# Three small reorderings in a hybrid encoder layer: transposes ahead of their copies, normalised products two at a time, a norm factor left in PSUM

## The chip, the cores and the metric

The kernel runs on one core of a Trainium2 chip. A core has TensorE (matrix products, PE in the profile, its weight loads PEld), VectorE (DVE), ScalarE (ACT), GpSimd (POOL) and SyncE (SP, which here only issues transfers). TensorE writes to PSUM, eight banks of 128 partitions by 512 float32 values; VectorE and ScalarE read it there. All else lies in SBUF. Each engine works through its own queue in order, and semaphores make one wait for another. The metric is the device time of one execution in microseconds; lower is better.

## The reference

One encoder layer, batch 1, 512 positions, width 2048, all in float32:

```
xn   = rms_norm(x)                       # attn_norm_g
u_val, u_gate, q, k, v = split(xn @ w_in)
A    = silu(layer_norm(depthwise_conv31(u_val * sigmoid(u_gate))))   # 1024 channels
B    = neighbourhood attention(q, k, v)  # 16 heads of 64, 8 x 64 grid, window 8 x 16, learned bias
x    = x + concat(rms_norm(A), rms_norm(B)) @ w_out
up   = depthwise_conv3(rms_norm(x) @ w_up)        # 2 x 5632 channels
gate, val = split(up)
x    = x + (silu(gate) * val) @ w_down
out  = rms_norm(x) * final_norm_g
```

## The kernel before

Activations lie transposed: a tile holds 128 channels by 512 positions. A product in float32 accuracy is made of three on rounded parts: each operand is split into a high part (a ScalarE copy that rounds) and a low part (a VectorE subtraction), and `mm3` issues high x high (L131), high x low (L135) and low x high (L136) into one PSUM bank. Weights come as raw units of 128 x 1024, are split by `parts` (L117 on ScalarE, L121 on VectorE), and are prepared three units ahead of their use.

The program is traced in Python, and a planner then puts each engine's instructions into a fixed order: among those that its own timing takes as ready, the one traced first goes first. `pin` (keep in program order) ties an instruction behind the one traced before it on its engine. Banks and buffers are handed out by tag; a new tile waits until the readers of the buffer's last tile are done.

The stages that matter, in order:

1. The input projections (`project`, tiles named `pj`), in the order that `ORDER` gives. After each group of eight k-steps `tick` advances a generator of side work by one step. One generator, `attention`, takes two heads (a pair) at a time: load tables, scores, softmax, then `turn`, then, two steps on, `values`.
2. `turn(ts)` transposes the pair's 16 blocks of 128 x 128 softmax values on TensorE (L537), in four groups of four. Groups 2 and 3 go to a bank each of tag `tr`, groups 0 and 1 to the two halves (one bank each) of one wide tile of tag `sc`. Behind each group ScalarE copies its bank to SBUF (L542). There are eight turns. The first `mm3` traced after a turn is pinned behind it.
3. The output projection runs in two halves, `out_half(ma, read_a)` over the convolution group and `out_half(mb, after)` over attention's, 16 output tiles of 24 products each. In the first half `read_a` multiplies each finished tile by the group's norm factor (L637, tile `oa`, from PSUM) and adds it to the residual (L638). Three PSUM banks of tag `mm` take turns, so a tile's bank must be read before the third tile after it begins.
4. `norm_b` is a generator that runs on the ticks of that first half. From attention's sum of squares it makes the factor `rna` through `factor` and `spread`, and then for each of the eight tiles `i` multiplies `aos[i]` by it (L627) and splits the result into `mb` (L170 on ScalarE, L171 on VectorE). It yields once, behind `i == 4`. The second half needs all eight, from its first output tile on.
5. The gated MLP in a fast matrix product scheme (tiles `pu`), 44 hidden tiles; this is most of the time. Down products (`pd`) are added to the residual in DRAM.
6. The tail. The last residual tiles `x2` are finished for the first 384 positions (`fm`), with sums of squares in `acc`. `spread(..., "rstd3", ...)` rounds and splits `acc` (L195, L196), sums it over channels by two products with ones (L200, bank of tag `po`, named `st`), and makes the factor by a root on ScalarE (L204) and three VectorE steps (L205, L206, L207). The last step writes `rstd` in SBUF. Meanwhile TensorE makes the last 128 positions with tokens on partitions, four banks `pt` of 512 columns (L1055, L1061, L1065, L1068); each is squared and summed on ScalarE (L1071), and its gain multiplied in on VectorE (L1077).
7. `along(g, k)` is called beside these products. At (1, 0), behind that step's first product, it runs the second part of `spread`; from then on each call hands out two pairs of output tiles to `finish`. Pairs 1, 4 and 7 go through ScalarE (gain, L1014) and GpSimd (factor, L1015, stored as a pair by L1021); the five others through one VectorE instruction a tile, x times gain times factor (L1017, each tile stored by L1019). The stores stand in SP's queue in program order.
8. When the fourth square sum is there, a chain of small instructions (L1079 to L1083) makes the factor for the last 128 positions, four column blocks `xg` are scaled and stored (L1091), and the program ends.

Of the kernel before, what the change touches and what calls it, by code (L numbers as in the profile page):

```python
# [10 lines left out]
F32 = mybir.dt.float32  # L11
F32R = mybir.dt.float32r
AF = mybir.ActivationFunctionType
ALU = mybir.AluOpType
AX = mybir.AxisListType

P = 128
D = 2048
# [14 lines left out]
NP_ = HEADS // 2  # L33
# [33 lines left out]
def layer(ctx: ExitStack, tc: tile.TileContext, xT, xG, xw, w_a, w_in, w_v, w_out, w_up, w_down, par, tab, g3, out, last_out):  # L67
    nc = tc.nc
# [6 lines left out]
    psa = ctx.enter_context(tc.tile_pool(name="psa", bufs=1, space=bass.MemoryType.PSUM))  # L75
# [9 lines left out]
    def t2(name, dt=F32):  # L85
        return tp.tile([P, S], dt, tag="t2k", name=name)

    def t4(shape, name):

        return wpool.tile(shape, F32, tag="raw", name=name, bufs=NR)  # L90

    pin = tc.keep_in_program_order
# [5 lines left out]
    def pc(name, i):  # L98
        o = POFF[name] + i
        return prm[:, o:o + 1]  # L100
# [66 lines left out]
    def split(src, g, name):  # L167

        h, l = t2(name + "h", F32R), t2(name + "l", F32R)
        nc.scalar.activation(h, src, AF.Copy, scale=g)  # L170
        nc.vector.scalar_tensor_tensor(l, src, g, h.bitcast(F32), op0=ALU.mult, op1=ALU.subtract)  # L171
        return h, l
# [15 lines left out]
        nc.vector.tensor_mul(y, y, v)  # L188
        nc.vector.scalar_tensor_tensor(y, y, 1.5, r, op0=ALU.add, op1=ALU.mult)

    def spread(acc, to, n, name, bank, hold=False):

        m = to.stop - to.start
        h, l = (t2("n" + c, F32R)[:, :m] for c in "hl")
        nc.scalar.activation(h, acc[:, to], AF.Copy)  # L195
        nc.vector.tensor_sub(l, acc[:, to], h.bitcast(F32))  # L196
        yield
        ps = bank()[:, :m]
        for i, x in enumerate((h, l)):
            x = nc.tensor.matmul(ps, ones_r, x, start=i == 0, stop=i == 1)  # L200
            if hold:
                pin(x)
        r, q = t2(name)[:, :m], t2("q")[:, :m]
        nc.scalar.activation(r, ps, AF.Abs_reciprocal_sqrt, scale=1.0 / n, bias=eps)  # L204
        nc.vector.scalar_tensor_tensor(q, r, -0.5 / n, r, op0=ALU.mult, op1=ALU.mult)  # L205
        nc.vector.scalar_tensor_tensor(q, ps, n * EPS, q, op0=ALU.add, op1=ALU.mult)  # L206
        nc.vector.scalar_tensor_tensor(r, q, 1.5, r, op0=ALU.add, op1=ALU.mult)  # L207
        return r

# [5 lines left out]
    def factor(acc, n, name, rest=1, free=False):  # L215
        steps = spread(acc, slice(0, S), n, name, lambda: stat_bank(free))
        next(steps)
        for _ in range(rest):
            yield
        try:  # L220
            next(steps)
        except StopIteration as e:
            return e.value
# [39 lines left out]
    ps = psa.tile([P, 2, S], F32, tag="sc", name="idle")  # L263
# [3 lines left out]
    for k in range(KD):  # L267
        if k < CH:
            raw = t4([P, U * P], "raw")
            n = S + 2 * P + (0 if k else KD)  # L270
# [3 lines left out]
        else:  # L274
            if k % CH == 0:
                raw = t4([P, U * P], "raw")
            if k % CH == 0 or k == CH + 2:
                o, n = 2 * (k % CH) * P, 2 * (2 if k < 2 * CH else CH) * P
# [4 lines left out]
        g = g1[:, k:k + 1] if k else raw[:, n - KD:n - KD + 1]  # L283
# [17 lines left out]
    for step in ORDER:  # L301
# [5 lines left out]
        i = next(a_ if step == "a" else q_)  # L307
# [220 lines left out]

    def turn(ts):
        pts, first = {}, True  # L530
        for n in (2, 3, 0, 1):
            if n == 0:
                wide = psa.tile([P, 2, 4, P], F32, tag="sc", name="trp")
            ps = wide[:, n] if n < 2 else psa.tile([P, 4, P], F32, tag="tr", name="trp", bufs=2)
            for i in range(2):
                for ch in range(2):
                    m = nc.tensor.transpose(ps[:, 2 * i + ch, :], ts[n][:, i, ch * P:(ch + 1) * P], ident)  # L537
                    if not first:
                        pin(m)
                    first = False  # L540
            pts[n] = t2("pt").rearrange("p (c k) -> p c k", c=4)
            nc.scalar.activation(pts[n], ps, AF.Copy)  # L542
        turned.append(pts)
        return pts
# [19 lines left out]
    def attention():  # L564

        before = None
        for p in range(NP_):
            while len(qk) <= p:
                yield
            ts = tables(p)  # L570
            yield
            if before:
                values(*before)
            banks = scores(p, not before)
            softmax(banks, ts)
            yield
            yield
            yield
            pts = turn(ts)
            yield  # L580
            before = p, pts
        yield
        values(*before)

    p, n = -1, 0
# [38 lines left out]
    def norm_b():  # L624
        r = yield from factor(acc_na, NA, "rna")
        for i in range(NP_):
            nc.vector.tensor_mul(aos[i], aos[i], r)  # L627
            mb.append(split(aos[i], pc("nag", i), "mb"))
            if i == NP_ // 2:
                yield  # L630

    def read_a(d, ps):
        wait.append((d, ps))
        while ra and wait:
# [3 lines left out]
            nc.vector.tensor_add(x2[d], x2[d], t)  # L638

    steps.append(norm_b())  # L640
    assert len(ma) == NC_
    out_half(ma, read_a)
# [333 lines left out]
    n = CH  # L976
# [28 lines left out]
    fm, tm = slice(0, LT), slice(LT, S)  # L1005

    def finish(pair, r, apart=False, split=False):

        o = t4([P, 2, LT], "fin")
        for i in range(2):  # L1010
            d = 2 * pair + i
            x, g = x2[d][:, fm], pc("g3", d)
            if apart:
                nc.scalar.activation(x, x, AF.Copy, scale=g)  # L1014
                nc.gpsimd.tensor_mul(o[:, i], x, r)  # L1015
            else:
                nc.vector.scalar_tensor_tensor(o[:, i], x, g, r, op0=ALU.mult, op1=ALU.mult)  # L1017
            if split:
                nc.sync.dma_start(out[pair][:, i], o[:, i])  # L1019
        if not split:  # L1020
            nc.sync.dma_start(out[pair], o)  # L1021

    acc = t2("acc3")
    for d in range(KD):
        ps = psm.tile([P, S], F32, tag="mm", name="pd")[:, fm]
        for k in range(n):
            mm3(ps, ws[d // CH * CH + k], d % CH, hs[k][0][:, fm], hs[k][1][:, fm], k == 0, k == n - 1)
        i = nc.vector.tensor_add(x2[d][:, fm], x2[d][:, fm], ps)
# [2 lines left out]
                pin(nc.scalar.activation(idle, eps, AF.Abs_reciprocal_sqrt))  # L1031
        sum_sq(acc[:, fm], x2[d][:, fm], d == 0, to=fm)

    rows = spread(acc, fm, D, "rstd3", stat_bank, hold=True)
    next(rows)
    wide = psa.tile([P, 2, S], F32, tag="sc", name="pt")
    banks = [psa.tile([P, S], F32, tag="tr", name="pt", bufs=2) if g % 2 else wide[:, g // 2] for g in range(CH)]
    rb, xg = [], []
    sums, v, r, y, w = (sm.tile([P, CH], F32, tag="rs" + c, name="rs" + c) for c in "lvryw")
    v, r, y, w = (t[:, :1] for t in (v, r, y, w))  # L1040
    pairs = list(range(KD // 2))

    def along(g, k):
        if (g, k) == (1, 0):
            try:
                next(rows)
            except StopIteration as e:
                rb.append(e.value)
        for at in pairs[:2 if rb else 0]:
            pairs.remove(at)  # L1050
            finish(at, rb[0], at % 3 == 1, at % 3 != 1)

    for g, ps in enumerate(banks):
        for i in range(CH):
            m = nc.tensor.matmul(ps[:, i * P:(i + 1) * P], x2[g * CH + i][:, tm], ident, start=i == 0, stop=False,  # L1055
                                 is_transpose=True)
            if g > 1 and i == 0:
                pin(m)
        for k in range(n):
            (hh, hl), (dh, dl) = hs[k], ws[g * CH + k]  # L1060
            i = nc.tensor.matmul(ps, hh[:, tm], dh, start=False, stop=False)  # L1061
            if (g, k) == (1, 0):
                pin(i)
                along(g, k)
            i = nc.tensor.matmul(ps, hl[:, tm], dh, start=False, stop=False)  # L1065
            if (g, k) == (1, 0):
                pin(i)
            nc.tensor.matmul(ps, hh[:, tm], dl, start=False, stop=k == n - 1)  # L1068
            if (g, k) != (1, 0):
                along(g, k)  # L1070
        nc.scalar.activation(t2("sq"), ps, AF.Square, accum_out=sums[:, g:g + 1])  # L1071
        if g == CH - 2:
            nc.vector.tensor_reduce(v, sums[:, :CH - 1], axis=AX.X, op=ALU.add)
            nc.vector.tensor_scalar(v, v, 1.0 / D, EPS, op0=ALU.mult, op1=ALU.add)
        xg.append(t2("xg"))
        if g < CH - 1:
            nc.vector.tensor_mul(xg[g], ps, gains[g])  # L1077
# [91 lines left out]
```

## Time and profile before

| | us |
|---|---|
| median of three runs | 2032.06 (2030.57 to 2032.34) |
| the profiled execution | 2031.56 |
| its span | 2029.8 |
| TensorE busy | 2008.3 |
| VectorE busy | 1672.3 |
| ScalarE busy | 1052.8 |
| GpSimd busy | 170.5 |
| granted TensorE clock, mean | 0.998 |

The span is the stretch that the profiler's records cover; the execution's own time is 1.8 us longer. A busy row counts the time in which an engine had an instruction under way; TensorE's products overlap, so its share says that it never stood still, not that it ran at its peak. In a timeline row the first number is the start, the second the time until the end of the last of the grouped instructions, `x12` their count, and the bracket the idle time just before with the instruction that ended it. In a row of waits the three numbers are the total, the count and the longest.

### The profile page before, as it was taken

The page shows a single profiled execution, that of the slowest core. Times are in us where ns is not written, and L with a number is a line of the kernel's source. Part 1 is how long each engine was busy: PE and PEld are TensorE (multiplying, and loading weights), DVE is VectorE, ACT ScalarE, POOL GpSimd, SP SyncE. Part 2 cuts the span into 40 slices and gives each one's busy share as a digit, 9 for nine tenths or more (in the row PEclk, how much of TensorE's full clock was granted, in tenths as well). Part 3 has the DMA queues.
Part 4 walks back from the last instruction along what each step waited for, and adds up shares of the span by engine and source line. Part 5 has one row for each costly group of instructions (what it writes and reads, how often), then busy time and mean ns, then how long its engine had stood idle before and what let it go on. Part 6 is the DMA issues. An engine that isn't in the chain of part 4 may idle for free.

```text
span 2029.8 us, 28055 instructions
## 1 busy us (share of the span) xinstructions
PE 2008.3 (99%) x10518; PEld 1715.8 (85%) x10518; DVE 1672.3 (82%) x2269; ACT 1052.8 (52%) x1688; POOL 170.5 (8%) x199
## 2 busy tenths in 40 slices
PE   9999999999999999999999999999999999999997
PEld 7888888888778998888888888888888888888887
DVE  7986888987577899888888888788888888889876
ACT  6323334476346655555555555555555555555563
POOL 0000000000001101111111111111111111110111
PEclk9999999999999999999999999999999999999999
DMA  7232323336338765566565565555566565555583
GB/s 256 83 104 91 115 88 106 110 126 214 99 109 221 188 178 145 125 146 145 125 145 145 134 136 146 135 135 145 125 145 146 125 145 146 135 136 135 135 219 113
DMA packets 98935, 284.25 MB, mean 140 GB/s; under 512 B 10992, under 2 KB 12272, under 8 KB 98800
## 3 DMA queue, kind: packets, MB, share of 16 engines
q1 hardware_dynamic: 72144, 231.07, 36.7%
q0 software_dynamic: 26656, 51.39, 17.0%
q8 instruction: 83, 1.36, 0.3%
q14 instruction: 52, 0.43, 0.1%
HBM read 227.89 MB, written 54.53 MB: 139 GB/s over the span
## 4 chain that ended last, share of the span: by engine, by line
PE 97%; DVE 1%; ACT 1%; DMA 0%; issue 0%; ACTq 0%; DVEq 0%
PE pu L791 26%; PE pu L797 14%; PE pd L136 8%; PE pd L131 8%; PE pd L135 8%; PE pj L131 6%; PE pj L135 6%; PE pj L136 6%; PE po L131 3%; PE po L135 3%; PE po L136 3%; PE pv L361 1%; PE pv L360 1%; PE pv L362 1%; PE po L553 1%; PE pu L135 1%
## 5 line engine op out<-in xcount | busy, mean ns | idle before, releaser
L117 ACT ACTIVATE whi<-raw 128x1024 fp32r<-128x1024 f32 x364 | 384.4, 1058 | 492.5 <-PE pj L135 125.4
L121 DVE TENSOR_TENSOR wlo<-raw,whi 128x1024 fp32r<-128x1024 f32 x364 | 444.7, 1223 | 207.7 <-ACT whi L117 199.1
L791 PE MATMUL pu<-xc,whi 128*128 128x512 f32 x2352 | 580.0, 391 | 0.0
L791 PEld LDWEIGHTS pu<-xc,whi 128*128 128x128 f32 x2352 | 433.5, 188 | 83.0
L797 PEld LDWEIGHTS pu<-xc,wlo 128*128 128x128 f32 x2352 | 306.8, 191 | 14.6
L797 PE MATMUL pu<-xc,wlo 128*128 128x256 f32 x2352 | 311.3, 283 | 0.0
L136 PE MATMUL pd<-hh,wlo 128*128 128x512 f32 x640 | 250.3, 391 | 0.0
L131 PE MATMUL pd<-hh,whi 128*128 128x512 f32 x640 | 249.6, 390 | 0.0
L135 PE MATMUL pd<-hl,whi 128*128 128x512 f32 x640 | 249.1, 389 | 0.0
L945 POOL DMA_DIRECT2D x2d<-pdc x160 | 139.3, 872 | 1097.4 <-ACT pdc L944 869.6
L131 PE MATMUL pj<-xh,whi 128*128 128x512 f32 x512 | 198.4, 392 | 0.3 <-ACT g L297 0.3
L135 PE MATMUL pj<-xl,whi 128*128 128x512 f32 x512 | 198.3, 390 | 0.0
L136 PE MATMUL pj<-xh,wlo 128*128 128x512 f32 x512 | 198.2, 390 | 0.0
L823 ACT ACTIVATE pl<-pu 128x256 f32<-128x256 f32 x294 | 109.7, 381 | 149.5 <-PE pu L791 142.6
L117 ACT ACTIVATE whi<-ws 128x1024 fp32r<-128x1024 f32 x132 | 139.8, 1059 | 73.9 <-PE pu L791 54.0
L416 DVE SCALAR_TENSOR_TENSOR y<-ch,prm,y 128x500 f32<-128x500 f32 (+14 forms) x240 | 173.6, 742 | 4.3
L121 DVE TENSOR_TENSOR wlo<-ws,whi 128x1024 fp32r<-128x1024 f32 x132 | 161.3, 1222 | 14.5 <-ACT whi L117 14.5
L136 PEld LDWEIGHTS pd<-hh,wlo 128*128 128x128 f32 x640 | 120.1, 188 | 28.4 <-DVE wlo L121 3.3
L135 PEld LDWEIGHTS pd<-hl,whi 128*128 128x128 f32 x640 | 120.2, 188 | 24.9 <-DVE hl L930 0.3
L131 PEld LDWEIGHTS pd<-hh,whi 128*128 128x128 f32 x640 | 120.4, 188 | 22.7
L944 ACT ACTIVATE pdc<-pd 128x512 f32<-128x512 f32 x160 | 93.8, 588 | 79.0 <-PE pd L136 65.9
L131 PEld LDWEIGHTS pj<-xh,whi 128*128 128x128 f32 x512 | 96.0, 188 | 21.4 <-ACT g L297 0.5
(237 smaller groups left out, 2730.3 us busy)
## 6 DMA issues: line engine op xcount, KB each, us to landing
raw<-in_w_up SPq DMA_DIRECT2D x176, 512.0 KB, 3.8
raw<-in_w_down SPq DMA_DIRECT2D x88, 512.0 KB, 3.9
x2d<-pdc POOLq DMA_DIRECT2D x160, 256.0 KB, 4.9
raw<-in_w_in SPq DMA_DIRECT2D x60, 512.0 KB, 3.8
raw<-in_w_out SPq DMA_DIRECT2D x32, 512.0 KB, 3.8
raw<-in_w_v SPq DMA_DIRECT2D x16, 512.0 KB, 3.8
tab<-in_tab SPq DMA_DIRECT2D x32, 256.0 KB, 5.2
x<-in_xT SPq DMA_DIRECT2D x16, 256.0 KB, 6.0
```

What stands on the lines that cost most here:

```text
L117: i = nc.scalar.activation(hi[:, :n], raw[:, :n], AF.Copy)
L121: j = nc.vector.tensor_sub(lo[:, :n], raw[:, :n], hi[:, :n].bitcast(F32))
L131: m = nc.tensor.matmul(ps, hi[:, a], mh, start=start, stop=False)
L135: nc.tensor.matmul(ps, hi[:, a], ml, start=False, stop=False)
L136: return nc.tensor.matmul(ps, lo[:, a], mh, start=False, stop=stop)
L360: nc.tensor.matmul(ps, xh, wh[:, f], start=kk == 0, stop=False)
L416: nc.vector.scalar_tensor_tensor(y[:, a:b], h[:, a + j - PAD:b + j - PAD], prm[:, o + j:o + j + 1], y[:, a:b], op0=ALU.mult, op1=ALU.add)
L791: i = nc.tensor.matmul(ps, w[0][:, k * P:(k + 1) * P], comb[c][k], start=k == 0, stop=stop and k == ks[-1])
L797: i = nc.tensor.matmul(ps[:, H:], w[1][:, k * P:(k + 1) * P], comb[c][k][:, :H], start=False, stop=stop and k == U - 1)
L823: nc.scalar.activation(to, ps, AF.Copy)
L944: nc.scalar.activation(t, ps, AF.Copy)
L945: nc.gpsimd.dma_start(xd[d], t, accum_op=ALU.add)
```

## The change

Three edits, in four functions.

- `turn` takes all four banks first and traces the sixteen transposes of the pair, still in the groups' order 2, 3, 0, 1, and only then the four copies.
- `norm_b` yields behind every second tile instead of once behind `i == 4`; the eight tiles are traced over four ticks.
- `spread` gets a flag `both`. With it, its last VectorE step writes the factor over the sums in PSUM, and ScalarE copies it to `r` in SBUF; both are returned. The tail's `finish` takes the PSUM one for VectorE's pairs and the SBUF one for GpSimd's. `along(1, 0)` is called ahead of that step's first product instead of behind it, so the two sums are traced ahead of all three products, of which only the first is still pinned.

```diff
-    def spread(acc, to, n, name, bank, hold=False):
+    def spread(acc, to, n, name, bank, hold=False, both=False):
...
         nc.vector.scalar_tensor_tensor(q, ps, n * EPS, q, op0=ALU.add, op1=ALU.mult)
+        if both:
+            nc.vector.scalar_tensor_tensor(ps, q, 1.5, r, op0=ALU.add, op1=ALU.mult)
+            nc.scalar.activation(r, ps, AF.Copy)
+            return ps, r
         nc.vector.scalar_tensor_tensor(r, q, 1.5, r, op0=ALU.add, op1=ALU.mult)
         return r
...
     def turn(ts):
         pts, first = {}, True
-        for n in (2, 3, 0, 1):
-            if n == 0:
-                wide = psa.tile([P, 2, 4, P], F32, tag="sc", name="trp")
-            ps = wide[:, n] if n < 2 else psa.tile([P, 4, P], F32, tag="tr", name="trp", bufs=2)
+        banks = [psa.tile([P, 4, P], F32, tag="tr", name="trp", bufs=2) for _ in range(2)]
+        wide = psa.tile([P, 2, 4, P], F32, tag="sc", name="trp")
+        banks += [wide[:, 0], wide[:, 1]]
+        order = (2, 3, 0, 1)
+        for n, ps in zip(order, banks):
             for i in range(2):
                 for ch in range(2):
                     m = nc.tensor.transpose(ps[:, 2 * i + ch, :], ts[n][:, i, ch * P:(ch + 1) * P], ident)
                     if not first:
                         pin(m)
                     first = False
+        for n, ps in zip(order, banks):
             pts[n] = t2("pt").rearrange("p (c k) -> p c k", c=4)
             nc.scalar.activation(pts[n], ps, AF.Copy)
...
             mb.append(split(aos[i], pc("nag", i), "mb"))
-            if i == NP_ // 2:
+            if i % 2:
                 yield
...
-    rows = spread(acc, fm, D, "rstd3", stat_bank, hold=True)
+    rows = spread(acc, fm, D, "rstd3", stat_bank, hold=True, both=True)
...
-                rb.append(e.value)
+                rb.extend(e.value)
         for at in pairs[:2 if rb else 0]:
             pairs.remove(at)
-            finish(at, rb[0], at % 3 == 1, at % 3 != 1)
+            finish(at, rb[at % 3 == 1], at % 3 == 1, at % 3 != 1)
...
         for k in range(n):
             (hh, hl), (dh, dl) = hs[k], ws[g * CH + k]
+            if (g, k) == (1, 0):
+                along(g, k)
             i = nc.tensor.matmul(ps, hh[:, tm], dh, start=False, stop=False)
             if (g, k) == (1, 0):
                 pin(i)
-                along(g, k)
-            i = nc.tensor.matmul(ps, hl[:, tm], dh, start=False, stop=False)
-            if (g, k) == (1, 0):
-                pin(i)
+            nc.tensor.matmul(ps, hl[:, tm], dh, start=False, stop=False)
             nc.tensor.matmul(ps, hh[:, tm], dl, start=False, stop=k == n - 1)
```

## The prediction

> **What bounds the kernel now.** I read the page's busy shares first, then the chain that ended last, then TensorE's own waits, then the timeline around each of them.
>
> ```profile
> span 2029.8 us, 28055 instructions
> PE 2008.3 (99%) x10518; PEld 1715.8 (85%) x10518; DVE 1672.3 (82%) x2269; ACT 1052.8 (52%) x1688; POOL 170.5 (8%) x199
> PE 97%; DVE 1%; ACT 1%; DMA 0%; issue 0%; ACTq 0%; DVEq 0%
> ...
> PE trp L537 <- ACT pt L542: 6.2, 6, 1.1
> PE po L131 <- DVE oa L637: 2.4, 2, 2.0
> ...
> 650.00:1950.00 1300.00, 1300.00 (x6976) 1125.69 (x6975) 1102.85 (x1415) 724.09 (x1130) 144.63 (x166) 1.00 0.60 143
> ```
>
> TensorE is the bound: 97% of the chain, without a gap from 650 to 1950 us (last row: PE, weight loads, VectorE, ScalarE, GpSimd, clock, DMA share, GB/s). It stops in few places, and the change works on three: behind the copies of the transposes (6.2 us in 6 waits), behind the read of a product (2.4 us in 2), and in the tail, where the store of the last columns ends the span.
>
> **Part one, the transposes.** One turn that waits, and one that does not:
>
> ```profile
> 254.34 1.47 PE L537 MATMUL trp<-ident,tab 128*128 128x128 f32 x12
> 255.27 1.55 ACT L542 ACTIVATE pt<-trp 128x512 f32<-128x512 f32 x3
> 256.88 0.66 PE L537 MATMUL trp<-ident,tab 128*128 128x128 f32 x4 [1.07 <-ACT pt L542]
> 257.29 0.49 PE L131 MATMUL pj<-xh,whi 128*128 128x512 f32 x1
> 257.57 0.60 ACT L542 ACTIVATE pt<-trp 128x512 f32<-128x512 f32 x1 [0.75 <-PE trp L537]
> ...
> 405.20 1.47 PE L537 MATMUL trp<-ident,tab 128*128 128x128 f32 x12
> 406.43 0.48 PE L131 MATMUL pj<-xh,whi 128*128 128x512 f32 x1
> 407.73 0.66 PE L537 MATMUL trp<-ident,tab 128*128 128x128 f32 x4
> 408.15 0.48 PE L131 MATMUL pj<-xh,whi 128*128 128x512 f32 x1
> ```
>
> At 254 the last four transposes start 0.06 us after the third copy ends (255.27 + 1.55 = 256.82). They write the second half of the two-bank tile whose first half that copy reads, and nothing else on ScalarE concerns them. With all sixteen traced ahead of the copies, no transpose follows a read of its tile. Without a stop, twelve take 406.43 - 405.20 = 1.23 us and four 257.29 - 256.88 = 0.41, so a turn takes 1.64 instead of 257.29 - 254.34 = 2.95: 1.31 less where the quoted wait is 1.07, 0.24 more than the wait itself. Over the six waits that is 6.2 + 6 x 0.24 = 7.6 us. In the two other turns (405 is one) other products fill the wait, and only a second switch between transposes and products goes: five products take 407.73 - 406.43 = 1.30 where five at 0.23 apart take 1.15, so 0.15 each. Part one: **7.9 us**.
>
> On ScalarE the same four copies run. Even if the first had to wait for all sixteen (1.64 us, some 0.17 more for the last result), four at 0.52 would end 3.9 us after the turn's start; now the last ends at 257.57 + 0.60, 3.8 after. So the copies cost nothing; if they did come late, the values products that read them are a step, some 5 us, away. Instruction counts and queues of SP and POOL are untouched. What may come late next is VectorE, which is filled with convolution taps here:
>
> ```profile
> 400.00:450.00 50.00, 48.94 (x271) 40.48 (x270) 44.98 (x71) 33.05 (x60) 0.00 (x0) 1.00 0.35 109
> 405.83 0.69 DVE L422 TENSOR_TENSOR ysum<-ysum,y 128x512 f32<-128x512 f32 x1
> L433 PE MATMUL st<-yh,ones x1: 394/394/394, 411.7 to 411.7; 128*128 128x512 f32 x1
> ```
>
> By then TensorE will be three waits earlier, 3.9 us, so the sum over channels at 411.7 would run at 407.8. If the taps kept their time (406.5, then a rounding and a subtraction of 0.6 and 0.7), it could run at 407.8 too. That is a tie: the lower end of the gain is half of it, 4.0, if VectorE at 45 of 50 us holds this stretch back. I take the whole, as VectorE still idles 5 us in 50 and the last taps follow a projection that itself comes earlier.
>
> **Part two, the second half's products.**
>
> ```profile
> 573.37 0.39 PE L136 MATMUL po<-mah,wlo 128*128 128x512 f32 x1
> 575.75 0.50 PE L131 MATMUL po<-mah,whi 128*128 128x512 f32 x1 [1.99 <-DVE oa L637]
> 581.10 0.39 PE L136 MATMUL po<-mah,wlo 128*128 128x512 f32 x1
> 581.90 0.47 PE L131 MATMUL po<-mah,whi 128*128 128x512 f32 x1 [0.42 <-DVE oa L637]
> 587.47 0.39 PE L131 MATMUL po<-mbh,whi 128*128 128x512 f32 x1
> ...
> 567.47 1.90 DVE L627 TENSOR_TENSOR ao<-ao,rna 128x512 f32<-128x512 f32 x3
> 575.00 0.69 DVE L637 TENSOR_TENSOR oa<-po,ra 128x512 f32<-128x512 f32 x1
> 580.40 0.76 DVE L171 SCALAR_TENSOR_TENSOR mbl<-ao,prm,mbh 128x512 fp32r<-128x512 f32 x1
> ```
>
> VectorE runs the normalising products and splits of five tiles before it reads the finished output tile at 575.00, and TensorE waits for that bank. Products are 0.23 apart, so the stops cost 575.75 - 573.60 = 2.15 and 581.90 - 581.33 = 0.57, and the slower first products another 0.10 and 0.08: **2.9 us**. With two tiles a step, only 2 x 0.60 + 2 x 0.66 = 2.5 us stand ahead of that read, which ends near 570.6, before the bank is wanted at 573.6; the next, after two more tiles, near 574.3, before 579.1. The work is the same, spread from two steps over four of the first half's last tiles. Price of the delay: four reads and sums more (4 x 0.60) come ahead of the last split, which moves from 581.2 to 583.5, or 584.7 with a weight split ahead too. The second half would begin at 587.47 - 2.9 = 584.6 and wants its eighth tile 21 products later, at 589.4: covered by 4.7 us. Ends: 0, if the planner places the reads late again, and 2.9; I take 2.9.
>
> **Part three, the tail.**
>
> ```profile
> 2008.86 0.34 PE L200 MATMUL st<-nh,ones 128*128 128x384 f32 x1
> 2009.10 0.69 DVE L1077 TENSOR_TENSOR xg<-pt,g3b 128x512 f32<-128x512 f32 x1 [0.63 <-ACT sq L1071]
> 2010.02 0.56 DVE L205 SCALAR_TENSOR_TENSOR q<-rstd 128x384 f32<-128x384 f32 x1 [0.23 <-ACT rstd L204]
> 2010.62 0.56 DVE L206 SCALAR_TENSOR_TENSOR q<-st,q 128x384 f32<-128x384 f32 x1
> 2011.80 9.91 DVE L1017 SCALAR_TENSOR_TENSOR fin<-x,prm,rstd 128x384 f32<-128x384 f32 x10
> 2011.91 7.80 POOL L1015 TENSOR_TENSOR fin<-x,rstd 128x384 f32<-128x384 f32 x6 [37.23 <-DVE rstd L207]
> L1017 DVE SCALAR_TENSOR_TENSOR fin<-x,prm,rstd x10: 605/1350/1374, 2011.8 to 2021.1; 128x384 f32<-128x384 f32 x10
> 2018.33 0.60 ACT L1071 ACTIVATE sq<-pt 128x512 f32<-128x512 f32 x1 [2.52 <-PE pt L1068]
> 2023.14 0.16 DVE L1079 SCALAR_TENSOR_TENSOR rsv<-rsl,rsv 128x1 f32<-128x1 f32 x1
> 2020.00:2021.00 1.00, 0.00 (x0) 0.00 (x0) 1.00 (x3) 0.00 (x0) 0.00 (x0) 1.00 1.05 404
> 2027.00:2028.00 1.00, 0.00 (x0) 0.00 (x0) 0.00 (x0) 0.00 (x0) 0.00 (x0) 0.50 1.04 389
> out_T<-fin SPq DMA_DIRECT2D x10, 192.0 KB, 2.1
> ```
>
> Of VectorE's ten output products the fast take 0.605 us, and those that run beside GpSimd's six 1.35. ScalarE and TensorE are not slowed there, so the two engines share something on their operands' way. The change takes one of VectorE's two tensors from SBUF to PSUM. No row shows such a product beside GpSimd. Its ends are ten at 0.605 (6.05 us) and no change (9.9). I take the lower: the nearest row by operands, L206, reads PSUM and SBUF in 0.56, as L205 reads SBUF alone. GpSimd and VectorE each step by 1.3 while both run, so GpSimd alone would need some 1.3 - 0.6 = 0.7 a product (an estimate); if not, 1.3.
>
> [...]
>
> The sum matmuls move ahead of one product, some 0.3 us; VectorE, busy with L1077 to 2009.79, starts L205 at 2009.80 instead of 2010.02: 0.2 us. The write of the factor into PSUM has no row; between 0 and 0.1 more, taken as 0. Then 2011.57 + 10 x 0.605 = 2017.6, the two gained columns and small sums that now stand between 2021.63 and 2023.14 (1.4), and L1079 at 2019.1. It needs the last square sum too, which begins at 2018.33 and is read out by some 2019.1. Both engines would be there 4.0 us earlier.
>
> ScalarE's added copy (0.52, by the 384-wide rounding of the same tile) holds GpSimd until 2012.3 and the square sum behind it by 0.2, which nobody awaits. SP's stores stand in order: pair 4, GpSimd's, goes ahead of pairs 5 and 6. At 0.7 a product it is there by 2015.2; at 1.3 by 2017.5, and then four pairs and the last columns, 2.6 MB, are left for queues that move some 390 GB/s (the rows at 404 and 389): 6.7 us from 2018.5, to 2025.2. Today the bytes stop just after 2028 (last window row); 4.0 earlier is 2024.1. All 4.2 MB take 10.8 from 2013.3, an estimate from the 2.1 us to a store's landing: also 2024.1, a tie. So I take **3.5**, between 2.9 and 4.0; the lowest end of part three is 0.
>
> **Sum.** 7.9 + 2.9 + 3.5 = 14.3 us. The profiled execution took 2031.56 (span 2029.8, 1.8 around it): 2017.3. The median of the runs, 2032.06, is 0.5 above it: **2017.8 us**.
>
> **Rivals.**
> - GpSimd still holds VectorE up, because what they share does not depend on where the factor lies (the per-channel factor stays in SBUF as well). For it: 1.35 beside 0.605 is all that is seen. Part three is then 0.0: 2021.3.
> - VectorE takes over in the convolution stretch. For it: 45 of 50 us and the tie above; against it, the 5 us idle. Half of part one is lost: 2021.8.
> - The reorder does not remove the wait (the shared tile makes another one): 6.4 us remain, 2025.7. Against it: after sixteen transposes only the next pair's scores write these banks, far later.
> - Slower than before: the order of the long stage is planned anew from other times, and a product there comes to wait for a weight split once a hidden tile.
>
> ```profile
> L121 DVE TENSOR_TENSOR wlo<-ws,whi 128x1024 fp32r<-128x1024 f32 x132 | 161.3, 1222 | 14.5 <-ACT whi L117 14.5
> ```
>
> One split of 1.22 us in each of 44 hidden tiles is 53.7: 2071.5. It decides from 14.3 / 1.22 = 12 tiles on. For it, VectorE is busy 1103 of 1300 us there; against, TensorE never stops in that stretch, so there is slack at each tile.
>
> **How the numbers follow.** Chances: forecast 0.64, GpSimd 0.15, convolution 0.12, wait not removed 0.03, long stage 0.06. The range runs from 2015.5 (part three at 4.0, and a microsecond or two of switches that I did not count) to 2023.0, which takes in the first two rivals. A measurement of this kernel tells about 0.2%, 4 us, from no change. Faster than that: the first four, less 0.01, 0.93; slower 0.06, same 0.01.
>
> **What would show it.** Right: no wait of a transpose on a copy, sixteen in one row of 1.9 us; no wait of L131 on L637; ten output products of 0.6 us under GpSimd's, and L1079 about 4 us earlier relative to the last product. Wrong: output products still at 1.35; a new TensorE wait on VectorE near 408; gaps between 650 and 1950; a store queue that ends later than the engines.

## The result and the profile after

The changed kernel takes 2017.74 us (median of 6 runs, 2017.12 to 2018.02) where the kernel before takes 2031.91 in the same runs: a ratio of 0.993, 95% interval 0.9917 to 0.9943, so 14.2 us less. The prediction was 2017.8. Its profiled execution has a span of 2015.3 us, 14.5 below the 2029.8 of before.

From the page of the changed kernel, its first lines and the chain by engine:

```profile
span 2015.3 us, 28052 instructions
...
PE 2005.8 (100%) x10518; PEld 1716.7 (85%) x10518; DVE 1667.3 (83%) x2269; ACT 1053.6 (52%) x1689; POOL 168.5 (8%) x199
...
PE 100%; ACT 0%; DVE 0%; ACTq 0%; issue 0%; POOL 0%; DVEq 0%; POOLq 0%
```

Its TensorE waits, all of them:

```profile
engine line waited for: us in total, times, longest us
PE idle L269 <- POOL warm L103: 1.1, 1, 1.1
```

And its timeline at the three places (start, time to the last end, engine, line):

```profile
253.71 1.91 PE L542 MATMUL trp<-ident,tab 128*128 128x128 f32 x16
255.38 0.48 PE L131 MATMUL pj<-xh,whi 128*128 128x512 f32 x1
...
533.46 1.91 PE L542 MATMUL trp<-ident,tab 128*128 128x128 f32 x16
535.12 0.49 PE L131 MATMUL po<-mah,whi 128*128 128x512 f32 x1
...
562.70 0.69 DVE L643 TENSOR_TENSOR oa<-po,ra 128x512 f32<-128x512 f32 x1
565.08 0.39 PE L131 MATMUL po<-mah,whi 128*128 128x512 f32 x1
575.43 0.74 DVE L171 SCALAR_TENSOR_TENSOR mbl<-ao,prm,mbh 128x512 fp32r<-128x512 f32 x1
575.96 0.39 PE L131 MATMUL po<-mbh,whi 128*128 128x512 f32 x1
...
1993.97 0.39 PE L1069 MATMUL pt<-dh,hh 128*128 128x512 f32 x1
1999.53 0.57 DVE L208 SCALAR_TENSOR_TENSOR st<-q,rstd 128x384 f32<-128x384 f32 x1
2000.19 0.49 ACT L209 ACTIVATE rstd<-st 128x384 f32<-128x384 f32 x1 [1.88 <-DVE st L208]
2000.71 5.34 DVE L1023 SCALAR_TENSOR_TENSOR fin<-x,prm,st 128x384 f32<-128x384 f32 x10 [0.62 <-ACT rstd L209]
2000.76 5.89 POOL L1021 TENSOR_TENSOR fin<-x,rstd 128x384 f32<-128x384 f32 x6 [37.24 <-ACT rstd L209]
2006.47 0.39 PE L1073 MATMUL pt<-dl,hh 128*128 128x512 f32 x1
2007.62 0.16 DVE L1084 SCALAR_TENSOR_TENSOR rsv<-rsl,rsv 128x1 f32<-128x1 f32 x1 [0.25 <-ACT sq L1076]
2009.03 2.74 SPq L1096 DMA_DIRECT2D out_N<-xg  x4
```

(Line numbers have moved: the transposes are L542, the output products L1023 and L1021, the small sum behind the last square L1084. SPq rows give the issue of transfers on SP.) TensorE has only its wait at the program's start left. Sixteen transposes stand in one row, the output tile is read at 562.7 before its bank is wanted at 565.1, and the ten output products take 5.34 us instead of 9.91. Below, the tail is the last stretch of the table, from the first product with tokens on partitions to the end of the span, and the small sum is L1084 (L1079 before). Between the landmarks, the two profiled executions differ by this:

| stretch | before | after | less |
|---|---|---|---|
| span's start to the first turn | 254.34 | 253.71 | 0.63 |
| first turn to the product behind the eighth | 289.29 | 281.41 | 7.88 |
| from there to the second half's first product | 43.84 | 40.84 | 3.00 |
| from there to the tail's first product with tokens on partitions | 1417.95 | 1418.01 | -0.06 |
| from there to the end of the span | 24.38 | 21.33 | 3.05 |

The first row is no effect of the change: in the ten executions below the first turn starts between 253.7 and 254.4.

### The profile page after: what moved, and what is told of

Read it like the earlier page. It is cut to its first block, busy times and chain, and to the rows that moved or that the text cites. A ratio compares the mean times of both kernels' runs of the same rounds, so it can differ in the third digit from the quotient of the medians.

```text
span 2015.3 us, 28052 instructions
## 1 busy us (share of the span) xinstructions
PE 2005.8 (100%) x10518; PEld 1716.7 (85%) x10518; DVE 1667.3 (83%) x2269; ACT 1053.6 (52%) x1689; POOL 168.5 (8%) x199
## 4 chain that ended last, share of the span: by engine, by line
PE 100%; ACT 0%; DVE 0%; ACTq 0%; issue 0%; POOL 0%; DVEq 0%; POOLq 0%
PE pu L797 27%; PE pu L803 14%; PE pd L136 8%; PE pd L131 8%; PE pd L135 8%; PE pj L131 6%; PE pj L136 6%; PE pj L135 6%; PE po L131 3%; PE po L135 3%; PE po L136 3%; PE pv L364 1%; PE pv L366 1%; PE pv L365 1%; PE po L559 1%; PE trp L542 1%
## 5 line engine op out<-in xcount | busy, mean ns | idle before, releaser
L136 PEld LDWEIGHTS pj<-xh,wlo 128*128 128x128 f32 x512 | 96.1, 188 | 20.4 <-DVE wlo L262 0.2
```

The costliest lines, as they stand in the source:

```text
L136: return nc.tensor.matmul(ps, lo[:, a], mh, start=False, stop=stop)
```

## The experiments

**One part at a time.** Three kernels, each the one before with one of the edits.

```diff
 # e1: turn() as in the changed kernel, norm_b and the tail as before
 # e2
-            if i == NP_ // 2:
+            if i % 2:
 # e3: spread(both), along and finish as in the changed kernel, the rest as before
```

> Only the transposes are put ahead of their copies. If the three parts add up, this gives 7.9 us of the 14.2: 2024.0, with each of the eight turns 1.66 us from its first transpose to the next product, and the waits near 575 (2.1 and 0.6 us) and the output products at 1.35 us still there. If part of that gain came from the other edits or from a newly planned order, it is off 2024.0 by more than 1.5 us.

> Only the normalising products are handed out two tiles at a time. By the theory the two stops in the first half of the output projection go (2.72 us, and 0.18 in the first products behind them) and nothing else changes: 2029.0, with eight tiles' splits done some 2 to 3 us later than before and no stop at the second half's start. The rival is that the stop only moves to another bank or to the second half: 2031.9.

> Only the tail: the factor in PSUM for VectorE, copied for GpSimd, and the sums one product earlier. By the two traces the stretch from the first tail product to the end of the span shrinks from 24.4 to 21.3 us: 2028.9. The rival is that this stretch was short by the luck of one execution: 24.4 again, 2031.9.

Beside 2031.24 for the kernel before: e1 2023.28 (ratio 0.9961, interval 0.9946 to 0.9975), e2 2028.08 (0.9984, 0.9975 to 0.9993), e3 2028.70 (0.9985, 0.9976 to 0.9995). That is 8.0, 3.2 and 2.5 us, 13.7 together, which the intervals don't tell from the 14.2 of all three. The traces separate them more sharply. TensorE's waits in e1, e2 and e3:

```profile
PE po L131 <- DVE oa L639: 2.4, 2, 2.0
PE idle L265 <- POOL warm L103: 1.1, 1, 1.1
```

```profile
PE trp L537 <- ACT pt L542: 6.2, 6, 1.1
PE idle L265 <- POOL warm L103: 1.1, 1, 1.1
PE st L200 <- DVE nl L196: 0.2, 1, 0.2
```

```profile
PE trp L541 <- ACT pt L546: 6.2, 6, 1.1
PE po L131 <- DVE oa L641: 2.4, 2, 2.0
PE idle L269 <- POOL warm L103: 1.1, 1, 1.1
PE pj L131 <- ACT whi L261: 0.6, 1, 0.6
```

Each edit removes its own wait and leaves those of the other parts as they were. From the first turn to the second half's start, e1 takes 7.9 us less than before (325.2 against 333.1), e2 3.0 less, e3 the same within 0.1; the tail takes 24.4, 24.3 and 21.3 us. In the traces the gains add up, and none of them depends on another.

**Why the transposes waited.** The kernel before, in its own order, but with the two halves of the wide tile as two tiles of one bank each.

```diff
+    def two(name):
+        return [psa.tile([P, S], F32, tag="sc", name=name, bufs=2) for _ in range(2)]
...
-                wide = psa.tile([P, 2, 4, P], F32, tag="sc", name="trp")
-            ps = wide[:, n] if n < 2 else psa.tile([P, 4, P], F32, tag="tr", name="trp", bufs=2)
+                wide = [t.rearrange("p (c k) -> p c k", c=4) for t in two("trp")]
+            ps = wide[n] if n < 2 else psa.tile([P, 4, P], F32, tag="tr", name="trp", bufs=2)
```

(The other users of the tag get two tiles in the same way.)

> The kernel before, with its order of transposes and copies; only the two-bank tile is two tiles of a bank each. If the wait of the last four transposes came from the copy that reads the other half of their tile, it is gone here as well: turns of 1.66 us, 7.9 us less, 2024.0. The rival is that the order itself makes the wait (a transpose traced behind a copy waits for it whatever it writes): six waits of about 1.07 us, 2031.9.

It takes 2023.41 us (0.996, 0.9945 to 0.9975), as e1 does. TensorE's waits:

```profile
PE po L134 <- DVE oa L638: 2.4, 2, 2.0
PE idle L268 <- POOL warm L106: 1.1, 1, 1.1
```

Its first turn in the timeline:

```profile
254.11 1.91 PE L538 MATMUL trp<-ident,tab 128*128 128x128 f32 x16
```

The copies are still traced between the transposes, and no transpose waits, where six did before (6.2 us). So the wait was not one for data nor for a bank: the dependency was kept for the whole tile, and a write to one bank waited for a read of the other, up to 1.1 us. The change avoids it by order; another division into tiles avoids it too.

**Where the factor lies.** The changed kernel, with every engine's order kept; VectorE's products read the copy in SBUF.

```diff
-            finish(at, rb[at % 3 == 1], at % 3 == 1, at % 3 != 1)
+            finish(at, rb[1], at % 3 == 1, at % 3 != 1)
```

> The changed kernel, with VectorE's ten output products reading the factor's copy in SBUF; the order of every engine stays as it is. If it is the place of that operand that frees VectorE, the products beside GpSimd's take 1.35 us again and GpSimd's 1.3 instead of 1.01, the chain behind them starts some 4.5 us later, the stores no longer pile up (1 us back), and the time is 3.5 us above the changed kernel: 2021.2. If the earlier sums or the order of the tail did it, the products stay at 0.61 and the time at 2017.7.

2021.05 us (0.9947, 0.9932 to 0.9963), 3.3 above the changed kernel, and a tail of 24.8; that is 0.4 more than in the kernel before, because the products start 0.4 later in it, behind ScalarE's copy. The output products of the two engines in this run, and then in the changed kernel (min/median/max in ns):

```profile
L1023 DVE SCALAR_TENSOR_TENSOR fin<-x,prm,rstd x10: 604/1348/1376, 2001.0 to 2010.3; 128x384 f32<-128x384 f32 x10
L1021 POOL TENSOR_TENSOR fin<-x,rstd x6: 1306/1321/1447, 2001.0 to 2007.6; 128x384 f32<-128x384 f32 x6
```

```profile
L1023 DVE SCALAR_TENSOR_TENSOR fin<-x,prm,st x10: 608/609/615, 2000.7 to 2005.4; 128x384 f32<-128x384 f32 x10
L1021 POOL TENSOR_TENSOR fin<-x,rstd x6: 1006/1011/1020, 2000.8 to 2005.6; 128x384 f32<-128x384 f32 x6
```

One operand's place is the whole difference: both engines are slowed when VectorE's two tensors lie in SBUF (medians of 1348 and 1321 ns), neither when one lies in PSUM (609 and 1011). The gain factor, a column of one value a partition, stays in SBUF and does no harm: the 609 are with it.

**GpSimd alone.** The changed kernel without VectorE's ten products.

```diff
-                nc.vector.scalar_tensor_tensor(o[:, i], x, g, r, op0=ALU.mult, op1=ALU.mult)
-            if split:
-                nc.sync.dma_start(out[pair][:, i], o[:, i])
+            if split:
+                nc.sync.dma_start(out[pair][:, i], x)
```

> The changed kernel without VectorE's ten output products: those ten tiles are stored without norm factor and gain. GpSimd's six products then run alone. If 1.01 us is GpSimd's own pace, it stays at 1.01. If VectorE still slows it although one operand lies in PSUM, it falls towards the 0.7 that the prediction worked out. The time says nothing of the change, since ten tiles are stored earlier.

```profile
L1021 POOL TENSOR_TENSOR fin<-x,rstd x6: 999/1005/1020, 2001.1 to 2006.0; 128x384 f32<-128x384 f32 x6
```

1.0 us is GpSimd's own pace (one run, 2016.55 us). The 0.7 that the prediction worked out, by taking the two engines to alternate for their whole instructions, is wrong: where both are slowed (e5) they step by 1.3, less than 1.0 + 0.6, so they overlap in part.

**Whether the stores now bound the tail.** The changed kernel without the stores of the last two pairs.

```diff
-            if split:
+            if split and pair != 6:
...
-        if not split:
+        if not split and pair != 7:
```

> The changed kernel without the stores of the last two of the eight pairs of output tiles: 0.79 of 4.2 MB of output are not written. If the tail is now bound by the stores, the stretch from the last square sum's use to the end of the span falls from 7.7 us to the 6.7 of the kernel before, and the span by 1.0, to 2014.3; more cannot come, since the engines' own chain is next. If the longer stretch has another cause, it stays at 7.7.

The small sum and the issue of the last stores in this run, the same issue in the kernel before, and then transfer rows of the changed kernel (last two columns: share of the DMA engines, GB/s):

```profile
2008.18 0.16 DVE L1084 SCALAR_TENSOR_TENSOR rsv<-rsl,rsv 128x1 f32<-128x1 f32 x1 [0.25 <-ACT sq L1076]
2009.60 1.80 SPq L1096 DMA_DIRECT2D out_N<-xg  x4
```

```profile
2024.56 1.80 SPq L1091 DMA_DIRECT2D out_N<-xg  x4
```

```profile
2004.00:2005.00 1.00, 1.00 (x6) 0.82 (x6) 1.00 (x3) 0.38 (x2) 1.00 (x2) 1.00 1.00 379
...
2012.00:2013.00 1.00, 0.00 (x0) 0.00 (x0) 0.00 (x0) 0.00 (x0) 0.00 (x0) 0.50 1.02 383
```

The span ends at 2015.0 (one run, 2016.81 us), 6.8 us behind that sum, against 7.7 in the changed kernel and 6.7 before; the tail takes 20.5 instead of 21.3 (the span itself fell by only 0.3, since this execution reached the tail 0.6 later). The four last stores are issued in 1.80 us again instead of 2.74, and that makes the difference: from the end of that issue to the end of the span it is 3.4 to 3.6 us in all three. In e6, where SP issues no store of those ten tiles after 2000.8, the span also ends 6.7 us behind the sum (2007.97 to 2014.7), though all the bytes are written. So the stores that have piled up do hold back the last ones after the change: the queues move some 380 GB/s from 2004 to 2013, and cost 0.9 to 1.0 us of what the engines gained.

**Without VectorE's wait for the copy.** VectorE's first output product waits 0.62 us for ScalarE's copy, though both only read the bank. No data ask for this wait; what does, no run here shows. In e8 a second VectorE step makes GpSimd's form instead (`shifted(4)` lets the planner place it a little later than it is traced).

```diff
             nc.vector.scalar_tensor_tensor(ps, q, 1.5, r, op0=ALU.add, op1=ALU.mult)
-            nc.scalar.activation(r, ps, AF.Copy)
-            return ps, r
+            with shifted(4): nc.vector.scalar_tensor_tensor(q, q, 1.5, r, op0=ALU.add, op1=ALU.mult)
+            return ps, q
```

> The changed kernel, with GpSimd's form of the factor made by a second VectorE step behind VectorE's first output product, instead of ScalarE's copy. VectorE's wait of 0.62 us on that copy is gone, so the first store goes out 0.6 us earlier; GpSimd starts 0.6 later. If the stores bound the tail, the stretch from the first tail product to the end falls from 21.3 us by 0.3 to 0.6, to 2017.3 in time; if GpSimd's later start holds SP's queue up instead, nothing is gained or up to 0.5 lost.

The step came to stand behind the first two products, not one, so GpSimd started 1.75 us behind VectorE's first product (2002.37 against 2000.62), where the two start together in the changed kernel. The time is 2018.72 (0.9935, 0.9923 to 0.9948), the tail 22.4: 1.1 lost, more than the expectation allowed for. Its store queue, and then that of the changed kernel:

```profile
2001.26 0.87 SPq L1025 DMA_DIRECT2D out_T<-fin  x2
2004.38 0.33 SPq L1027 DMA_DIRECT2D out_T<-fin  x1
2004.81 1.95 SPq L1025 DMA_DIRECT2D out_T<-fin  x4
```

```profile
2001.35 1.13 SPq L1025 DMA_DIRECT2D out_T<-fin  x2
2002.78 0.33 SPq L1027 DMA_DIRECT2D out_T<-fin  x1
2003.21 1.98 SPq L1025 DMA_DIRECT2D out_T<-fin  x4
```

The wait is gone and the first store is 0.58 earlier against the tail's first product (1994.46 there). But the queue then stands until 2004.38 for GpSimd's first pair, with two finished tiles of VectorE behind it and a third just ending. That pair's store is 1.11 us later than in the changed kernel, as much as the tail is longer. Run e10 keeps e8's step and puts two more of VectorE's stores ahead of that pair's:

```diff
-    pairs = list(range(KD // 2))
+    pairs = [0, 2, 1, 3, 5, 4, 6, 7]
```

> The second VectorE step stands, as in the run before it, behind VectorE's first two output products; the pairs are handed out in the order 0, 2, 1, 3, 5, 4, 6, 7, so that SP has two stores more ahead of GpSimd's first pair. If the 1.1 us that the run before lost came from SP waiting for that pair with VectorE's tiles behind it, the stretch from the first tail product to the end falls from 22.4 us to between 20.9 and 21.4. If it came from GpSimd's later start alone, it stays above 22.

The tail is 21.3 again (one run, 2017.75 us), which puts e8's loss on the order in SP's queue. Run e9 turns the two forms round: VectorE writes SBUF, ScalarE copies into PSUM, and the first product alone reads SBUF (`d` is the tile's number).

```diff
-            nc.vector.scalar_tensor_tensor(ps, q, 1.5, r, op0=ALU.add, op1=ALU.mult)
-            nc.scalar.activation(r, ps, AF.Copy)
+            nc.vector.scalar_tensor_tensor(r, q, 1.5, r, op0=ALU.add, op1=ALU.mult)
+            nc.scalar.activation(ps, r, AF.Copy)
...
-                nc.vector.scalar_tensor_tensor(o[:, i], x, g, r, op0=ALU.mult, op1=ALU.mult)
+                nc.vector.scalar_tensor_tensor(o[:, i], x, g, r if d else rb[1], op0=ALU.mult, op1=ALU.mult)
```

> The changed kernel with the two forms of the factor made the other way round: VectorE writes SBUF, ScalarE copies it into PSUM, and VectorE's first output product alone reads the SBUF form. Then neither VectorE nor GpSimd waits for the copy, and the first store goes out 0.6 us earlier with GpSimd's pairs earlier too. If the store queue, fed from its first store on, bounds the tail, the stretch from the first tail product to the end falls from 21.3 us to 20.7, and the time to 2017.1; if it is bound by the engines' chain behind the last product, it stays at 21.3.

2017.14 us (0.9928, 0.9914 to 0.9941) with a tail of 21.15. GpSimd's six products, the small sum and two rows of the store queue in this run:

```profile
L1021 POOL TENSOR_TENSOR fin<-x,rstd x6: 1002/1018/1387, 2000.8 to 2006.2; 128x384 f32<-128x384 f32 x6
2008.20 0.16 DVE L1084 SCALAR_TENSOR_TENSOR rsv<-rsl,rsv 128x1 f32<-128x1 f32 x1 [0.83 <-ACT sq L1076]
2003.20 0.33 SPq L1027 DMA_DIRECT2D out_T<-fin  x1
2009.61 2.57 SPq L1096 DMA_DIRECT2D out_N<-xg  x4
```

Neither VectorE's first product nor GpSimd's waits for the copy, and the first store is 0.58 earlier, but only 0.2 of it reaches the end: it is neither the 20.7 nor quite the 21.3. The other 0.4 goes in the queue's stop for GpSimd's first pair, whose store is only 0.16 earlier against the tail's first product (1994.55 here): GpSimd's first product, beside the one product of VectorE that reads SBUF, takes 1.39 us. The tail follows that store, 0.18 shorter here and 1.11 longer in e8, while the small sum stands 13.65 us behind the tail's first product in the changed kernel, in e8 and in e9 alike. That e9 beats the changed kernel cannot be told from these runs (2016.76 to 2017.46 against 2017.12 to 2018.02, with starts that scatter by 0.7).

## Why the prediction was right, step by step

- **Part one.** Predicted 7.9, measured 7.88 in the stretch of the eight turns, and 8.0 as the only edit (e1). A turn takes 1.66 to 1.67 us where 1.64 was worked out. Its reason, the read of the tile's other half, was an inference from one end time; e4 shows it. The lower end, VectorE's taps holding TensorE back near 408, did not come: there is no wait there.
- **Part two.** Predicted 2.9, measured 3.00, and 3.2 as the only edit (e2). The read came 3.7 us after the first normalising product began, where 2.5 was worked out from two tiles ahead of it: VectorE took four products and two splits first. That was early enough. The last split ended at 576.2, 0.2 us after the second half began, the later of the two cases that the prediction gave (584.7 against 584.6); its tile is wanted 4.8 us into the half, so the cover is 4.6 us, as against 4.7.
- **Part three.** Predicted 3.5 between 2.9 and 4.0, measured 3.05 (2.5 in time as the only edit, e3). Its terms were less good than its sum. The ten products take 5.34 us, not 6.05: in a row without a stop they follow each other at 0.53. GpSimd's pace is 1.0, not 0.7. The wait of 0.62 for ScalarE's copy was not foreseen: the copy was charged to GpSimd and the square sum alone. The small sum stands 1.15 us behind TensorE's last product instead of 5.24, 4.1 earlier, as predicted (4.0). But VectorE's row, for which those terms were added up, does not set it: the sum waits 0.25 us for ScalarE's last square sum, the other side of what the prediction had as a tie at 2019.1, and it stands at the same place in e9, where VectorE's wait is gone. So the errors on VectorE cost nothing. Then the stores take back 1.0, where the prediction let them take 0.5. The term that was mis-sized is the store queue, also a tie in the prediction; e7 shows that it is the bound. A store queue that ends later than the engines was among the prediction's signs of being wrong, and it came, but cost only that.
- **The 0.2 us of the earlier sums** came: L205 starts 4.37 us after the tail's first product instead of 4.60. No run tests it alone; VectorE had 0.25 us to spare before the small sum.
- **The total** agrees to 0.1 us partly by luck: the four stretches behind the first turn give 13.9 us where 14.3 was added up, and the medians of the kernel before differ by 0.7 from one set of runs to another (2031.24 to 2031.98).
- **The place of the operand.** That VectorE goes unslowed beside GpSimd once one of its two tensors lies in PSUM was the author's estimate; no row before the change showed such a pair. The changed kernel shows it at 0.61 us a product, and e5 the other case, 1.35 with both in SBUF. A cost of the PSUM operand itself does not appear: 609 ns with it, 604 without it and without contention (e5's shortest).
- **The rival on the other side**, a wait for weight splits in the long stage, did not come: that stretch changed by 0.06 us of 1418.

## What to carry to other kernels

Where a bound engine stops for about a microsecond at the same place of every round, look which instruction's end it starts behind, and whether the two touch the same bytes or only the same tile; order (e1) or smaller tiles (e4) took the wait away here, 6.2 us of it. In a generator of side work, count what stands between a finished product and the read that frees its bank. A store queue in program order can stand at the next tile in it, as in e8 until 2004.38 with two finished tiles behind: look which engine makes that one. When two engines slow each other, look at where each operand lies (here 1.35 against 0.61 us a product), and when a tail gets shorter on the engines, ask what its transfers need: here they took back a quarter of the 4.1 us.

## What the runs showed of the hardware

- A 128x384 VectorE product takes 0.61 us with one tensor in PSUM, beside GpSimd or not (603 to 615 ns in e8, where two of the ten stand before GpSimd's first), and 1.35 with both in SBUF while GpSimd multiplies two tensors in SBUF. GpSimd's own goes from 1.0 to 1.3. Neither blocks the other for a whole instruction: that would make 1.6.
- Stores from SBUF run at some 380 GB/s while the DMA share of the windows is 1.01 to 1.04 (369 to 388 from 2005 to 2013 in the changed kernel). The issues on SP grow there as well, to as much as 0.91 us where most took 0.33 in the kernel before (the ten single-tile stores' shortest was 0.34, their median 0.43).
